# Down product of a two-layer encoder: the VectorE work of the Strassen items queued in the order of the program text

## The chip, the cores and the metric

The kernel runs on one core of a Trainium2 chip. The metric is the device time of one execution in microseconds (us). Before the change the median of 3 runs is 2260.68 us (2259.78 to 2261.06).

## The reference, cut to what matters

The reference is a trunk of two layers, each a mixer (an mLSTM, then a latent attention) and an MLP with a squared ReLU, on 1024 tokens of width 1024 in float32. The change lies in the second matrix product of the MLP:

```python
D_MODEL, SEQ, DEPTH = 1024, 1024, 2
D_FF = 4 * D_MODEL

def sq_relu_mlp(h, w1, w2):
    return jnp.square(jax.nn.relu(h @ w1)) @ w2

for layer in range(DEPTH):
    ...
    y = sq_relu_mlp(h, ffn_w1[layer], ffn_w2[layer])
    x = x + g2[:, None, :] * rms_norm(y, norm_g[layer, 3])
```

Here `h @ w1` is the up product (1024 x 1024 by 1024 x 4096) and the multiplication by `w2` (4096 x 1024) the down product. The trace shows one down product at about 801 to 1110 us and the other at about 1921 to 2258 us.

## The kernel before

**Three matmuls for one.** Every float32 operand is cut into a high part (an ACT cast, `uh`, `whi`) and a low part (a VectorE subtraction of the high part from the original, `ul`, `wlo`). `mm3` issues three matmuls of 128x128 by 128x512 for each product of tiles: high by high (L168), low weights by high activations (L169), and high weights by low activations (L170).

**Strassen items.** `mlp` (from L774) does the down product in 32 items: 8 groups `g` of two pairs of weight tiles each (`GP` = 2), and in each group 4 row blocks `j`. The first 28 items use a Strassen scheme of seven products, the last 4 (the group `ng - 1`) plain products. The products of an item come in the order s = 1, 6, 2, 3, 5, 4, 7 (loop variable `n`). Products 1 and 6 fill the two halves of one PSUM tile "mm" (128x1024), 2 and 3 the next, 4 and 7 the third; product 5 goes to a tile "sm" (128x512) that stays in PSUM for each `j` from the first group to the last and is never added on the way. Each "mm" tile takes 12 matmuls, product 5 takes 6, so an item has 42.

**Accumulators.** For each `j` there are three tiles "y" in SBUF: `c16`, `c23`, `c47`. After products 6, 3 and 7 `add` (L814) adds the "mm" tile into its accumulator: a VectorE addition of 128x1024 (L819), or an ACT copy (L817) in the first group. The pool of "mm" tiles has two buffers, so the matmuls of a tile cannot begin before the addition of the tile two before it has read the buffer.

**Activations.** `load` brings the tiles `u` of an item two items ahead; `cut_high` (L807, ACT) makes `uh` of the next item after product 1, `cut_low` (L813, two VectorE subtractions) makes `ul` after product 6.

**Weights.** The weights of later groups are prepared by generators (`w_pair` from L580, `w_plain` from L563 for the last group), which `w_step` moves on by one step after each product as long as room for tiles is left. For one pair of weight tiles the steps issue four GpSimd additions (L611, L612, L624, L631), ACT casts (L600, L636), three VectorE subtractions `wlo` (L604), and one VectorE subtraction for the tile `w4` of product 4 (L638). In `w_plain` the VectorE subtraction is L574.

**What sets the order.** A scheduler of the framework orders the instructions of each engine by a simulated timeline; a block under `tc.issue_after(X)` stays behind instruction X in the queue. Before the change only `cut_low` was held so: behind the instruction traced last, whichever it was. A helper `behind(*engines)` exists already; it looks up the last traced instruction of each engine named and holds what is traced in its block behind it. Additions, `wlo`, `w4` and the combining additions after the last Strassen group (L885, seven for each `j` when `g == ng - 2`) were ordered by the scheduler alone.

Of the kernel before, what the change touches and what calls it, by code (L numbers as in the profile page):

```python
# [65 lines left out]
class Trunk:  # L66
# [711 lines left out]
    def mlp(self, l, done, extra, last=None):  # L778

        S, V, G, GP, NP = self.S, self.V, self.G, self.GP, self.NP  # L780
# [5 lines left out]
        def load(it):  # L786
            if it < items:
                g, j = divmod(it, 4)
                loaded[it] = []
                for i in range(GP):  # L790
                    src = self.us[g * GP + i].rearrange("p (o j t) -> p o j t", o=8, j=4)[:, :, j]
                    if g == ng - 1:
                        if i == 0:
                            u = self.U("u")[:, : GP * 512]
                            loaded[it].append(u)
                        self.dma(out=u[:, i * 512 : (i + 1) * 512].rearrange("p (o t) -> p o t", o=4), in_=src[:, :4])
                    else:
                        u = self.U("u")[:, :896]
                        loaded[it].append(u)
                        self.dma(out=u.rearrange("p (o t) -> p o t", o=7), in_=src[:, 1:])  # L800

        def cut_high(it):
            if it < items:
                cuts[it] = []
                for u in loaded[it]:
                    x = tuple(v[:, : u.shape[-1]] for v in (self.U("uh", F32R), self.U("ul", F32R)))
                    S.copy(x[0], u)  # L807
                    cuts[it].append(x)

        def cut_low(it):  # L810
            if it < items:
                for u, x in zip(loaded.pop(it), cuts[it]):
                    V.tensor_tensor(out=x[1], in0=u, in1=x[0].bitcast(F32), op=ALU.subtract)  # L813

        def add(dst, ps, fresh=False):
            if fresh:
                S.copy(dst, ps)  # L817
            else:
                V.tensor_tensor(out=dst, in0=dst, in1=ps, op=ALU.add)  # L819
# [25 lines left out]
        for it in range(items - 4):  # L845
            g, j = divmod(it, 4)
            load(it + 2)
            c23, c47, c16 = acc[j]
            for n, (s, half) in enumerate(((1, 0), (6, 1), (2, 0), (3, 1), (5, None), (4, 0), (7, 1))):
                if half == 0:  # L850
                    both = self.MM()
                if half is None and g == 0:
                        fives[j] = self.SM()
                ps = fives[j] if half is None else both[:, (lo, hi)[half]]
                o = (self.US.index(self.LEFT[s]) - 1) * P
                start, stop = half is not None or g == 0, half is not None or g == ng - 2
                for i in range(GP):
                    key = (1, g * GP + i)
                    self.mm3(ps, tuple(u[:, o : o + P] for u in cuts[it][i]), self.w_take(key, s), start and i == 0, stop and i == GP - 1)
                    if j == 3:  # L860
                        self.w_used(key, s)
                if s == 6:
                    add(c16, both, g == 0)
                elif s == 3:
                    add(c23, both, g == 0)
                elif s == 7:
                    add(c47, both, g == 0)
                if n == 0:
                    cut_high(it + 1)
                elif n == 1:  # L870
                    with self.tc.issue_after(self.last()):
                        cut_low(it + 1)
                self.w_step(room=self.ROOM[1])
            del cuts[it]
            if g == ng - 2:
                for dst, src in (
                    (c16[:, hi], c16[:, lo]),
                    (c23[:, lo], c16[:, lo]),
                    (c47[:, hi], c16[:, hi]),
                    (c47[:, lo], c47[:, hi]),  # L880
                    (c47[:, hi], fives[j]),
                    (c16[:, hi], fives[j]),
                    (c23[:, hi], c16[:, hi]),
                ):
                    V.tensor_tensor(out=dst, in0=dst, in1=src, op=ALU.add)  # L885
                acc[j] = c23, c47
# [3 lines left out]
        for j in range(4):  # L890
# [3 lines left out]
            for row in (1, 0) if last and j == 3 else (0, 1):  # L894
                y = (even, odd)[row]
                both = self.MM()
# [1074 lines left out]
```

## Time and profile before

| What | Value |
|---|---|
| Median of 3 runs | 2260.68 us (2259.78 to 2261.06) |
| Profiled execution | 2259.8 us, of which span 2258.0 us |
| Mean granted TensorE clock | 0.996 |
| PE (TensorE matmuls) busy | 2200.4 us, 97% of the span |
| DVE (VectorE) busy | 1689.3 us, 75% |
| ACT (ScalarE) busy | 1013.2 us, 45% |
| POOL (GpSimd) busy | 458.1 us, 20% |

The profile comes from one execution. PE stands for TensorE's matmuls and PEld for its weight loads, DVE for VectorE, ACT for ScalarE, POOL for GpSimd, SP for the queue that issues DMAs. A line of a group names the line of the kernel, engine, operation, output and inputs, shapes, count, busy time in us, mean ns of one, and the idle time of the engine just before these instructions with what ended most of it. A line of the timeline gives start and duration in us, then the same names, "x2" for two in a row, and in brackets the idle time before and who ended it.

### The profile page before, as it was taken

The numbers are of one execution on the slowest core, as the hardware profiler recorded it, in microseconds if no ns is written. First come the engines' busy times: TensorE is split into PE (matmuls) and PEld (weight loads), VectorE is DVE, ScalarE is ACT, GpSimd is POOL, SyncE is SP. The second block draws the span as 40 slices with busy tenths as digits, with TensorE's granted clock in tenths as the row PEclk, the third lists the DMA queues.
The fourth block names the chain that finished last, engine by engine and source line by source line (L and its number), as shares of the span: only waits on it lengthen the run. The fifth ranks groups of instructions, "written<-read, shape, count | busy, mean of one in ns | idle before, by whom it ended". The sixth has DMA issues, their size and how long they took to land.

```text
span 2258.0 us, 28912 instructions
## 1 busy us (share of the span) xinstructions
PE 2200.4 (97%) x10814; PEld 1835.6 (81%) x10814; DVE 1689.3 (75%) x2503; ACT 1013.2 (45%) x1695; POOL 458.1 (20%) x309
## 2 busy tenths in 40 slices
PE   8999999999999999999999999999999999999998
PEld 6898888878778877777898989988787888777776
DVE  5677787567987768788988676664779776687888
ACT  4511445563444463333354445555634444633322
POOL 0000120004543434231000000000045433333300
PEclk9999999999999999999999999999999999999999
DMA  9487443245764554454321000113457545545452
GB/s 300 133 289 257 93 132 121 94 120 172 251 199 159 186 178 132 137 154 149 117 82 44 17 16 17 40 65 103 122 174 237 172 154 172 173 136 171 128 172 103
DMA packets 300068, 320.17 MB, mean 142 GB/s; under 512 B 16040, under 2 KB 252184, under 8 KB 299928
## 3 DMA queue, kind: packets, MB, share of 16 engines
q1 hardware_dynamic: 299928, 318.33, 44.7%
q8 instruction: 85, 1.39, 0.3%
q14 instruction: 55, 0.45, 0.1%
HBM read 245.85 MB, written 72.43 MB: 141 GB/s over the span
## 4 chain that ended last, share of the span: by engine, by line
PE 76%; DVE 14%; ACT 3%; issue 3%; DMA 3%; SPq 1%; DVEq 0%; POOL 0%; ACTq 0%; POOLq 0%
PE mm L168 14%; PE mm L170 14%; PE mm L169 14%; PE sm L168 10%; PE sm L169 10%; PE sm L170 10%; PE sm L208 3%; DVE wlo L604 2%; DVE ul L813 2%; DVE y L819 2%; DVE x L739 1%; DMA slab<-in_mod_w_dram 1%; DVE y L885 1%; DVE acc L298 1%; DMA modw<-in_mod_w_dram 1%
## 5 line engine op out<-in xcount | busy, mean ns | idle before, releaser
L168 PE MATMUL mm<-whi,uh 128*128 128x512 f32 x688 | 273.6, 398 | 14.5 <-DVE y L819 14.2
L169 PE MATMUL mm<-wlo,uh 128*128 128x512 f32 x688 | 271.0, 394 | 0.0
L170 PE MATMUL mm<-whi,ul 128*128 128x512 f32 x688 | 270.7, 394 | 0.0
L819 DVE TENSOR_TENSOR y<-y,mm 128x1024 f32<-128x1024 f32 (+1 forms) x161 | 192.6, 1208 | 86.3 <-PE mm L170 86.3
L631 POOL TENSOR_TENSOR tt<-raw,tt 128x512 f32<-128x512 f32 x60 | 113.6, 1893 | 616.4 <-DVE wlo L604 616.4
L168 PE MATMUL sm<-hSh,whi 128*128 128x512 f32 x560 | 223.0, 398 | 8.3 <-DVE x L739 8.0
L169 PE MATMUL sm<-hSl,whi 128*128 128x512 f32 x560 | 221.7, 396 | 0.0
L170 PE MATMUL sm<-hSh,wlo 128*128 128x512 f32 x560 | 219.9, 396 | 0.0
L739 DVE TENSOR_TENSOR x<-x,sm 128x512 f32<-128x512 f32 x198 | 132.3, 682 | 57.6 <-PE sm L170 54.3
L168 PEld LDWEIGHTS mm<-whi,uh 128*128 128x128 f32 x688 | 129.1, 188 | 53.7 <-DVE y L819 21.3
L813 DVE TENSOR_TENSOR ul<-u,uh 128x896 fp32r<-128x896 f32 (+1 forms) x120 | 153.5, 1318 | 24.9 <-ACT uh L807 24.9
L807 ACT CAST uh<-u 128x896 fp32r<-128x896 f32 (+1 forms) x120 | 109.6, 947 | 122.3 <-DVE ul L813 114.1
L611 POOL TENSOR_TENSOR tt<-raw,raw 128x512 f32<-128x512 f32 x32 | 64.8, 2025 | 486.0 <-DMA raw<-in_ffn_w_dram 480.2
L170 PEld LDWEIGHTS mm<-whi,ul 128*128 128x128 f32 x688 | 129.2, 188 | 30.3
L169 PEld LDWEIGHTS mm<-wlo,uh 128*128 128x128 f32 x688 | 129.2, 188 | 29.0
L604 DVE TENSOR_TENSOR wlo<-raw,whi 128x1024 fp32r<-128x1024 f32 x104 | 147.6, 1419 | 5.5 <-ACT whi L600 5.5
L168 PEld LDWEIGHTS sm<-hSh,whi 128*128 128x128 f32 x560 | 105.8, 189 | 36.4 <-DVE x L739 8.3
L742 ACT ACTIVATE x<-x 128x1024 f32<-128x1024 f32 x64 | 67.8, 1059 | 144.8 <-DVE x L739 144.5
L600 ACT CAST whi<-raw 128x1024 fp32r<-128x1024 f32 x104 | 108.7, 1045 | 42.7 <-DMA raw<-in_ffn_w_dram 21.3
L170 PEld LDWEIGHTS sm<-hSh,wlo 128*128 128x128 f32 x560 | 105.9, 189 | 25.1
L169 PEld LDWEIGHTS sm<-hSl,whi 128*128 128x128 f32 x560 | 105.9, 189 | 24.3
L298 DVE SCALAR_TENSOR_TENSOR acc<-modw,cact,acc 128x1024 f32<-128x1024 f32 x84 | 115.3, 1373 | 3.5 <-DMA modw<-in_mod_w_dram 2.6
(428 smaller groups left out, 5717.0 us busy)
## 6 DMA issues: line engine op xcount, KB each, us to landing
raw<-in_ffn_w_dram SPq DMA_DIRECT2D x144, 512.0 KB
u<-us SPq DMA_DIRECT2D x112, 448.0 KB
us<-x SPq DMA_DIRECT2D x92, 512.0 KB
modw<-in_mod_w_dram SPq DMA_DIRECT2D x80, 512.0 KB
x<-xn SPq DMA_DIRECT2D x24, 512.0 KB
x<-x SPq DMA_DIRECT2D x24, 512.0 KB
x<-in_x_dram SPq DMA_DIRECT2D x16, 512.0 KB
slab<-in_mod_w_dram SPq DMA_DIRECT2D x32, 256.0 KB
```

The source lines that it names most:

```text
L168: mm(out, a[0], b[0], start=start, stop=False)
L169: mm(out, a[0], b[1], start=False, stop=False)
L170: mm(out, a[1], b[0], start=False, stop=stop)
L298: self.V.scalar_tensor_tensor(out=acc, in0=t, scalar=self.cact[:, k : k + 1], in1=acc, op0=ALU.mult, op1=ALU.add)
L600: S.copy(x[0], u)
L604: V.tensor_tensor(out=x[1], in0=u, in1=x[0].bitcast(F32), op=ALU.subtract)
L631: G.tensor_tensor(out=t1, in0=b21, in1=t2, op=ALU.subtract)
L739: V.tensor_tensor(out=dst, in0=src, in1=ps, op=ALU.add)
L742: S.activation(u, u, AF.Relu)
L807: S.copy(x[0], u)
L813: V.tensor_tensor(out=x[1], in0=u, in1=x[0].bitcast(F32), op=ALU.subtract)
L819: V.tensor_tensor(out=dst, in0=dst, in1=ps, op=ALU.add)
```

## The change

The additions of the products, `cut_low`, and the step of the weight preparation after each product are all put under `behind(V)`, V being VectorE. Each block's VectorE instructions thereby stand in VectorE's queue behind the VectorE instruction that was traced last before the block. The instructions and their sizes stay the same; so do the additions at L885 themselves, which have no block of their own (they are at L887 afterwards, since two lines are added above them).

```diff
-                if s == 6:
-                    add(c16, both, g == 0)
-                elif s == 3:
-                    add(c23, both, g == 0)
-                elif s == 7:
-                    add(c47, both, g == 0)
+                with self.behind(V):
+                    if s == 6:
+                        add(c16, both, g == 0)
+                    elif s == 3:
+                        add(c23, both, g == 0)
+                    elif s == 7:
+                        add(c47, both, g == 0)
                 if n == 0:
                     cut_high(it + 1)
                 elif n == 1:
-                    with self.tc.issue_after(self.last()):
+                    with self.behind(V):
                         cut_low(it + 1)
-                self.w_step(room=self.ROOM[1])
+                with self.behind(V):
+                    self.w_step(room=self.ROOM[1])
```

VectorE's queue where one group ends and the next begins (item j = 3 of a group in the middle of the first layer, then j = 0 of the next group). The accumulators are y_1156 (`c23` of j = 3), y_1157 (`c47` of j = 3), y_1149 (`c16` of j = 0); mm_1267, mm_1272 and mm_1277 are the PSUM tiles of these three, in the order of their use:

```order
+L819 TENSOR_TENSOR y_1156_6934<-y_1156_6934,mm_1267_7468 128x1024
 L604 TENSOR_TENSOR wlo_1249_7353<-raw_1234_7291,whi_1248_7352 128x1024
 L604 TENSOR_TENSOR wlo_1269_7491<-tt_1247_7349,whi_1268_7490 128x1024
+L819 TENSOR_TENSOR y_1157_6935<-y_1157_6935,mm_1272_7497 128x1024
 L604 TENSOR_TENSOR wlo_1274_7505<-raw_1233_7289,whi_1273_7504 128x1024
-L819 TENSOR_TENSOR y_1156_6934<-y_1156_6934,mm_1267_7468 128x1024
-L819 TENSOR_TENSOR y_1157_6935<-y_1157_6935,mm_1272_7497 128x1024
-L638 TENSOR_TENSOR w4_1282_7534<-tt_1247_7349,w4_1282_7534 128x512
 L819 TENSOR_TENSOR y_1149_6927<-y_1149_6927,mm_1277_7521 128x1024
 L813 TENSOR_TENSOR ul_1279_7529<-u_1260_7442,uh_1278_7528 128x896
 L813 TENSOR_TENSOR ul_1281_7532<-u_1261_7444,uh_1280_7531 128x896
+L638 TENSOR_TENSOR w4_1282_7534<-tt_1247_7349,w4_1282_7534 128x512
```

The `c23` addition has moved ahead of three `wlo` subtractions and the `c47` addition ahead of one, and `w4` has moved behind the `c16` addition and the two `ul`. After this piece the `c23` addition of j = 0 (mm_1283) now stands ahead of wlo_1286 instead of behind it, and the `c47` addition (mm_1291) ahead of wlo_1293 instead of behind it.

TensorE's queue at the same place: mm_1277 is the tile of products 1 and 6 of j = 0, mm_1283 that of 2 and 3, mm_1291 that of 4 and 7 (from here the names end in further tiles of the two weight pairs):

```order
 L170 MATMUL mm_1283_7546<-whi_1248_7352,ul_1266_7457 128x512
+L169 MATMUL mm_1277_7521<-wlo_1274_7505,uh_1265_7456 128x512
+L170 MATMUL mm_1277_7521<-whi_1273_7504,ul_1266_7457 128x512
+L168 MATMUL mm_1277_7521<-whi_1231_7286,uh_1263_7453 128x512
+L169 MATMUL mm_1277_7521<-wlo_1232_7287,uh_1263_7453 128x512
+L170 MATMUL mm_1277_7521<-whi_1231_7286,ul_1264_7454 128x512
+L168 MATMUL mm_1277_7521<-whi_1268_7490,uh_1265_7456 128x512
+L169 MATMUL mm_1277_7521<-wlo_1269_7491,uh_1265_7456 128x512
+L170 MATMUL mm_1277_7521<-whi_1268_7490,ul_1266_7457 128x512
 L168 MATMUL mm_1291_7581<-w4_1245_7330,uh_1263_7453 128x512
 L169 MATMUL mm_1291_7581<-w4_1245_7330,uh_1263_7453 128x512
```

Before, these eight matmuls of mm_1277 stood ahead of the twelve of mm_1283; now they stand behind them and directly ahead of mm_1291, which uses the same PSUM buffer as mm_1277. Also, the four matmuls of product 5 of the next item that read its `ul` (sm_1191) stood behind all twelve of mm_1291 and now stand behind the first four of them. The full order from the tile of the ended item on is: before, mm_1272 x12, sm x6, mm_1277 x12, mm_1283 x12, mm_1291 x12, sm_1191 x4, mm_1296; after, mm_1272 x12, sm x2, mm_1277 x4, sm x4, mm_1283 x12, mm_1277 x8, mm_1291 x4, sm_1191 x4, mm_1291 x8, mm_1296.

VectorE's queue at the last Strassen group (j = 0), y_1149, y_1147 and y_1148 being `c16`, `c23` and `c47` of j = 0, y_1152 `c16` of j = 1:

```order
 L819 TENSOR_TENSOR y_1148_6926<-y_1148_6926,mm_1512_8726 128x1024
+L887 TENSOR_TENSOR y_1148_6926<-y_1148_6926,y_1149_6927 128x512
+L887 TENSOR_TENSOR y_1148_6926<-y_1148_6926 128x512
+L887 TENSOR_TENSOR y_1148_6926<-y_1148_6926,sm_1171_6988 128x512
+L887 TENSOR_TENSOR y_1149_6927<-y_1149_6927,sm_1171_6988 128x512
+L887 TENSOR_TENSOR y_1147_6925<-y_1147_6925,y_1149_6927 128x512
 L574 TENSOR_TENSOR wlo_1516_8745<-raw_1513_8733,whi_1515_8744 128x1024
-L887 TENSOR_TENSOR y_1147_6925<-y_1147_6925,y_1149_6927 128x512
-L887 TENSOR_TENSOR y_1148_6926<-y_1148_6926,y_1149_6927 128x512
 L819 TENSOR_TENSOR y_1152_6930<-y_1152_6930,mm_1519_8758 128x1024
```

Between the `c47` addition of j = 0 and the `c16` addition of j = 1 there stood one `wlo` and two combining additions; now five combining additions and the `wlo`. The order on ACT, POOL and SP is the same before and after.

## The prediction

> **What bounds the kernel now.** I read the busy times of the page first, then TensorE's list of waits over the whole run and over the first layer's down product (798 to 1112 us), then the stretches by engine, then the timelines of TensorE and VectorE at one place where a group of items ends.
>
> ```profile
> PE 2200.4 (97%) x10814; PEld 1835.6 (81%) x10814; DVE 1689.3 (75%) x2503; ACT 1013.2 (45%) x1695; POOL 458.1 (20%) x309
> L819 DVE TENSOR_TENSOR y<-y,mm 128x1024 f32<-128x1024 f32 (+1 forms) x161 | 192.6, 1208 | 86.3 <-PE mm L170 86.3
> ```
>
> ```profile
> PE mm L168 <- DVE y L819: 14.2, 17, 1.3
> ```
>
> ```profile
> PE mm L168 <- DVE y L819: 6.7, 8, 1.3
> PE mm L168 <- ACT y L817: 1.1, 1, 1.1
> ```
>
> TensorE is busy 97% of the span, so the change can only move TensorE's idle time. The change touches the down products alone, and there the waits are nearly all for the additions at L819 (in all 14.2 us in 17 waits; 6.7 us in 8 of them in the first layer). VectorE itself waits 86.3 us for matmuls in front of those additions, so it is not full on average, but the stretches show how much room it has:
>
> ```profile
> 964.00:1004.00 40.00, 39.21 (x168) 31.39 (x168) 32.12 (x29) 14.48 (x16) 13.10 (x9) 1.00 0.48 143
> 1044.00:1085.00 41.00, 38.29 (x162) 29.80 (x161) 39.59 (x46) 14.05 (x19) 0.90 (x1) 1.00 0.56 173
> ```
>
> The columns are the stretch, its length, then the busy time of PE, PEld, DVE, ACT and POOL, the granted clock, the DMA share and GB/s. A group of four items takes 40 us; VectorE works 32.12 us of it, TensorE 39.21. In the last Strassen group VectorE works 39.59 of 41 us: it is full there. Now the place where a group ends, first TensorE, then VectorE:
>
> ```profile
> 1002.10 0.40 PE L170 MATMUL mm<-whi,ul 128*128 128x512 f32 x1
> 1002.34 0.39 PE L170 MATMUL sm<-whi,ul 128*128 128x512 f32 x1
> ...
> 1003.50 0.40 PE L170 MATMUL sm<-whi,ul 128*128 128x512 f32 x1
> 1004.79 0.50 PE L168 MATMUL mm<-whi,uh 128*128 128x512 f32 x1 [0.90 <-DVE y L819]
> 1005.13 0.40 PE L169 MATMUL mm<-wlo,uh 128*128 128x512 f32 x1
> 1005.37 0.39 PE L170 MATMUL mm<-whi,ul 128*128 128x512 f32 x1
> ```
>
> ```profile
> 998.11 2.09 DVE L813 TENSOR_TENSOR ul<-u,uh 128x896 fp32r<-128x896 f32 x2
> 1000.12 1.22 DVE L604 TENSOR_TENSOR wlo<-raw,whi 128x1024 fp32r<-128x1024 f32 x1
> ...
> 1002.39 1.22 DVE L604 TENSOR_TENSOR wlo<-raw,whi 128x1024 fp32r<-128x1024 f32 x1
> 1003.52 2.35 DVE L819 TENSOR_TENSOR y<-y,mm 128x1024 f32<-128x1024 f32 x2
> 1005.79 0.77 DVE L638 TENSOR_TENSOR w<-tt,w 128x512 fp32r<-128x512 f32 x1
> 1007.88 1.22 DVE L819 TENSOR_TENSOR y<-y,mm 128x1024 f32<-128x1024 f32 x1 [1.33 <-PE mm L170]
> 1009.02 2.08 DVE L813 TENSOR_TENSOR ul<-u,uh 128x896 fp32r<-128x896 f32 x2
> ```
>
> The matmul at 1004.79 opens the next group's first tile and waits for the `c23` addition, which stands behind three `wlo` and ends at 1004.74. The down product of a layer has six ends of a group among its seven Strassen groups: the first (term 3), four of this kind (terms 1 and 2) and the last (term 4).
>
> **The step lengths.** From these rows: one matmul to the next 0.232 us (1002.34 to 1003.50 in five), but 0.34 after a stall; one addition or `wlo` to the next 1.13 (1000.12 to 1002.39 in two); an addition alone 1.22; two `ul` 2.01 (998.11 to 1000.12); a `w4` 0.77 alone (0.68 where an addition follows). TensorE starts 0.05 after the addition ends. How long after a tile's last matmul starts the addition does, shows this pair:
>
> ```profile
> 848.43 0.40 PE L170 MATMUL mm<-whi,ul 128*128 128x512 f32 x1
> ```
>
> ```profile
> 848.86 1.22 DVE L819 TENSOR_TENSOR y<-y,mm 128x1024 f32<-128x1024 f32 x1 [0.63 <-PE mm L170]
> 850.00 2.09 DVE L813 TENSOR_TENSOR ul<-u,uh 128x896 fp32r<-128x896 f32 x2
> ```
>
> 0.43 us. With these I replay the new order of the two queues by hand.
>
> **Term 1: the ordinary end of a group.** The new order does move the `c23` addition to 1000.12 (in front of the three `wlo`), and the first four matmuls of mm_1277 no longer wait. Ten matmuls then follow mm_1272 and the next, mm_1283, would start at 1002.34 + 10 x 0.232 = 1004.66. It needs the `c47` addition, now at 1000.12 + 3 x 1.13 = 1003.51, ended 1004.73: it starts at 1004.79, the very time of before. The last of its twelve starts at 1005.13 + 10 x 0.232 = 7.45 (from here us after 1000), the last of the eight of mm_1277 put behind it at 9.31. Then mm_1291 comes at once and needs mm_1277's buffer. The `c16` addition starts 9.31 + 0.43 = 9.74 and ends 10.96; mm_1291 would start at 9.54 and starts at 11.01: a wait of 1.47, with nothing between to hide it. Before, twelve matmuls (2.8 us) stood between the two tiles. Behind the addition stand the two `ul` (10.87 to 12.96), which product 5 of the next item needs after four plus three matmuls: wanted at 12.74, starts 13.01. Then `w4`, now last in the row, 12.88 to 13.65, which the next matmul of mm_1291 needs: wanted at 13.35, starts 13.70. With 0.11 for each restart mm_1291 ends its starts at 13.70 + 0.34 + 6 x 0.232 = 15.43, and mm_1296 opens at 15.66. Before it opened at 1005.13 + 39 x 0.232 = 14.18. So the end of a group costs **1.5 us more**, not less.
>
> **Term 2: what follows in the next item.** VectorE is late as well:
>
> ```profile
> 1017.15 1.22 DVE L819 TENSOR_TENSOR y<-y,mm 128x1024 f32<-128x1024 f32 x1 [0.38 <-PE mm L170]
> 1018.29 4.20 DVE L813 TENSOR_TENSOR ul<-u,uh 128x896 fp32r<-128x896 f32 x2
> 1022.41 0.68 DVE L638 TENSOR_TENSOR w<-tt,w 128x512 fp32r<-128x512 f32 x1
> 1023.01 2.34 DVE L819 TENSOR_TENSOR y<-y,mm 128x1024 f32<-128x1024 f32 x2
> ```
>
> ```profile
> 1024.40 0.39 PE L168 MATMUL mm<-whi,uh 128*128 128x512 f32 x1
> ```
>
> Before, the addition that frees the buffer of the matmul at 1024.40 ended at about 1024.2, just in time. After, `w4` at 12.88 is followed by `c23`, two `wlo`, `c47`, `wlo` and then the `c16` addition: 12.88 + 0.68 + 5 x 1.13 = 19.2 instead of 17.15. The same steps put the end of the `c23` addition at 24.2 + 2.05 = 26.25, where TensorE, 1.5 late, wants it at 25.9: a wait of 0.4 and a restart, some 0.5 us. Bounds: nothing, if the two `ul` (4.20 here, 2.09 above) are not slowed when they run later; and 1.1 more, if `w4` runs as in its slow row, 1.78 instead of 0.68:
>
> ```profile
> 857.67 3.19 DVE L813 TENSOR_TENSOR ul<-u,uh 128x896 fp32r<-128x896 f32 x2
> 860.79 1.78 DVE L638 TENSOR_TENSOR w<-tt,w 128x512 fp32r<-128x512 f32 x1
> 862.49 2.34 DVE L819 TENSOR_TENSOR y<-y,mm 128x1024 f32<-128x1024 f32 x2
> ```
>
> In both rows `ul` and `w4` together take 4.7 to 4.8 us, so I take the same again, **0.6**, with 0 and 1.7 as ends. Terms 1 and 2 apply to four ends of a group in each layer: 4 x 2.1 = 8.4.
>
> What slows the `ul` shows in GpSimd's rows of the same time:
>
> ```profile
> 1018.14 1.29 POOL L612 TENSOR_TENSOR tt<-raw,tt 128x512 f32<-128x512 f32 x1
> 1019.39 2.15 POOL L624 TENSOR_TENSOR raw<-raw,raw 128x512 f32<-128x512 f32 x1
> ```
>
> The first `ul` begins inside L612 and the second beside L624, and both stretch. GpSimd's additions follow the `wlo` and move with VectorE, so I leave the overlap as it is. [...]
>
> **Term 3: the first end of a group** (from ACT copies to additions). Before, `w4` and the `c23` addition were done ahead of the `c16` addition at 848.86; now `c16`, two `ul`, `w4`, `c23`. The next tile takes the buffer of the one that `c16` reads until 850.08: it starts at 850.13 instead of 849.13 (+1.0), then waits for `ul` at 852.1 (0.3) and for `w4` at 852.7 (0.3), with three restarts (0.3): **+1.9 us**. The stall that follows today at 863.75, behind the slow `w4` and the addition at 862.49, stays, both engines being as late as each other. Ends: 1.0 (the buffer alone) and 3.0 (`w4` slow as at 860.79).
>
> **Term 4: the last Strassen group.** The end of a group as in term 1, 1.5. Then the combining additions:
>
> ```profile
> L885 DVE TENSOR_TENSOR y<-y,y x24: 661/680/687, 1057.4 to 2211.8; 128x512 f32<-128x512 f32 x24
> ```
>
> ```profile
> 1066.46 1.21 DVE L819 TENSOR_TENSOR y<-y,mm 128x1024 f32<-128x1024 f32 x1
> 1067.59 1.88 DVE L885 TENSOR_TENSOR y<-y,y 128x512 f32<-128x512 f32 x3
> 1069.40 1.21 DVE L819 TENSOR_TENSOR y<-y,mm 128x1024 f32<-128x1024 f32 x1
> ```
>
> They follow one another in 0.60 us (1067.59 to 1069.40 in three). In the new order five instead of two stand ahead of the `c16` addition of j = 1, so it comes 1.8 us later, and VectorE has no room there (39.59 of 41). The replay through this group gives waits for additions of 0.6, 1.9, 0.5, 0.9 and 0.3 with five restarts of 0.11, 4.7 in all, where before there were four worth 2.9, the first and the last of them these:
>
> ```profile
> 1055.32 0.51 PE L168 MATMUL mm<-whi,uh 128*128 128x512 f32 x1 [0.38 <-DVE y L819]
> ...
> 1084.96 0.47 PE L168 MATMUL mm<-whi,uh 128*128 128x512 f32 x1 [1.34 <-DVE y L819]
> ```
>
> So 1.8 more, and **3.2** with the end of the group. Ends: 0.5 (VectorE's work is the same, so the group ends nearly when it did) and 5.
>
> The `w4` moved behind the `ul` at the start of the down product (804 to 813 us) I cost at nothing: TensorE waits there at 810 for the ACT copy at L817 in any case; without that cover it would be one `w4`, 0.7. The loads of `u` and GpSimd's work have two items of room. The four plain items are only shifted.
>
> **The sum.** Per layer 1.9 + 8.4 + 3.2 = 13.5, in two layers 27.0. On the profiled execution's own 2259.8 us that is 2286.8; the median of the runs is 0.9 above it, so 2288. With the low ends 1.0 + 4 x 1.5 + 0.5 = 7.5, twice 15: 2276. With the high ends 3.0 + 4 x 3.2 + 5 = 20.8, twice 41.6: 2302.
>
> **Rivals.**
> *Faster.* The additions come earlier and the waits for L819 go: 14.2 us with 17 restarts of 0.11 is 16.1, so 2244.6. For it: the `c23` addition does move from 1003.52 to 1000.12. Against it: it decides on whether 1.7 us of other matmuls (0.43 + 1.22 + 0.05) stand between mm_1277's last and mm_1291's first, and the order shows none. Chance 0.04.
> *No change.* TensorE has other matmuls in the waits, or the gain at `c23` is just given back: within 4.5 us of 2260.7. Against it: each engine's queue is in order. Chance 0.03.
> *A smaller loss.* Only term 1 holds, no wait in the next item, and the last group gives nothing: 2265 to 2276. Chance 0.10.
> *A larger loss.* VectorE, at 32 of 40 us a group, does not catch up in the three items behind a group's end, and the lateness is carried into the next end: if 1.5 us of it meets each of the eight next ends, 12 more, 2300; with slow `ul` and `w4` 2310. Chance 0.09. For it: term 2; against: VectorE has 8 us of idle time in a group.
>
> **How the numbers follow.** The forecast, 2276 to 2302 around 2288, has 0.74. A measurement of this kernel can tell about 0.2% (4.5 us) from no change. Faster is the first rival, 0.04; within 0.2% the second, 0.03; all the rest is slower, 0.93. The range is the forecast's own with 2 us more on each side, 2274 to 2304: it takes in the ends of the terms and part of the smaller and the larger loss, and leaves out some 0.2.
>
> **What would show it.** Right, if the profile after has, at each end of a group, TensorE waiting about 1.5 us for the `c16` addition (not `c23`), then short waits for `ul` L813 and `w4` L638, which do not occur now; if waits for L819 grow from 14.2 to some 30 us; and if in the last group `mm` waits stand behind runs of five L887. Term 2 is wrong if the matmul some 20 us after each end of a group does not wait. All of it is wrong if mm_1291 opens without a wait: then its buffer was another one. With all of TensorE's busy time unchanged (2200 us), any other difference must be in the clock, which is 1.00 in these stretches.

## The result and the profile after

The changed kernel takes 2289.14 us (median of 4 runs, 2287.77 to 2293.45), beside 2260.23 us for the kernel before in the same comparison: a ratio of 1.0131, 95% interval 1.0119 to 1.0142. The forecast was 2288 (2274 to 2304). The profiled execution took 2289.35 us with a span of 2287.5 us, 29.5 us more than the span before.

TensorE's list of waits of the changed kernel shows where the time is:

```profile
PE mm L168 <- DVE y L819: 29.3, 31, 2.3
PE sm L168 <- DVE x L739: 9.5, 10, 3.6
```

The waits for the additions have gone from 14.2 us in 17 to 29.3 us in 31. The next entry lies outside the down product; it was 8.0 us in 8 before the change.

The end of a group in the middle of the first layer (the same one as in the prediction; it now lies some 9 us later). TensorE's lines with a wait of at least 0.3 us:

```profile
1020.14 0.50 PE L168 MATMUL mm<-w,uh 128*128 128x512 f32 x1 [1.31 <-DVE y L819]
1035.69 0.50 PE L168 MATMUL mm<-whi,uh 128*128 128x512 f32 x1 [0.64 <-DVE y L819]
```

Two shorter waits follow the first of these, and the starts show them:

```profile
1021.71 0.40 PE L169 MATMUL sm<-wlo,uh 128*128 128x512 f32 x1
1022.14 0.50 PE L170 MATMUL sm<-whi,ul 128*128 128x512 f32 x1
1022.74 0.50 PE L169 MATMUL mm<-w,uh 128*128 128x512 f32 x1
```

VectorE at that place:

```profile
1018.86 1.22 DVE L819 TENSOR_TENSOR y<-y,mm 128x1024 f32<-128x1024 f32 x1 [3.69 <-PE mm L170]
1020.00 2.09 DVE L813 TENSOR_TENSOR ul<-u,uh 128x896 fp32r<-128x896 f32 x2
1022.00 0.68 DVE L638 TENSOR_TENSOR w<-tt,w 128x512 fp32r<-128x512 f32 x1
1022.60 1.22 DVE L819 TENSOR_TENSOR y<-y,mm 128x1024 f32<-128x1024 f32 x1
...
1028.46 1.21 DVE L819 TENSOR_TENSOR y<-y,mm 128x1024 f32<-128x1024 f32 x1
1029.60 3.20 DVE L813 TENSOR_TENSOR ul<-u,uh 128x896 fp32r<-128x896 f32 x2
1032.72 1.78 DVE L638 TENSOR_TENSOR w<-tt,w 128x512 fp32r<-128x512 f32 x1
1034.42 2.34 DVE L819 TENSOR_TENSOR y<-y,mm 128x1024 f32<-128x1024 f32 x2
```

The matmul at 1020.14 reads `w`, so it is the first of the tile of products 4 and 7, and it waits for the `c16` addition of 1018.86. VectorE waited 3.69 us in front of that addition, for TensorE: the addition could not start before the eight matmuls that the new order had put last. Each engine waits for the other in turn. The matmul at 1022.14 starts 0.05 us after the `ul` pair ends (1022.09), 0.43 us behind the matmul before it instead of 0.23, and the one at 1022.74 starts 0.06 after `w4` ends (1022.68), 0.60 behind. The matmul at 1035.69 waits for the first addition of 1034.42, behind an `ul` pair of 3.20 us and a `w4` of 1.78.

Stretches of the changed kernel (PE, PEld, DVE, ACT, POOL busy, granted clock, DMA share, GB/s):

```profile
1000.00:1040.00 40.00, 37.91 (x160) 29.09 (x159) 30.16 (x27) 13.77 (x15) 13.81 (x8) 1.00 0.47 145
1040.00:1080.00 40.00, 35.95 (x143) 27.08 (x142) 32.06 (x34) 14.08 (x16) 1.31 (x1) 0.96 0.41 125
```

In 40 us TensorE starts 160 matmuls instead of 168. VectorE is less busy than before (30.16 against 32.12): a group now takes 42.4 us instead of 40.1 (from the wait for `c16` at one end, 977.77, to that at the next, 1020.14), so less of its work falls into 40 us.

In the last Strassen group VectorE's lines around the combining additions are these:

```profile
1069.62 1.21 DVE L819 TENSOR_TENSOR y<-y,mm 128x1024 f32<-128x1024 f32 x1
1070.87 0.69 DVE L887 TENSOR_TENSOR y<-y,y 128x512 f32<-128x512 f32 x1
1071.59 0.69 DVE L887 TENSOR_TENSOR y<-y 128x512 f32<-128x512 f32 x1
1072.32 1.28 DVE L887 TENSOR_TENSOR y<-y,sm 128x512 f32<-128x512 f32 x2
1073.64 0.69 DVE L887 TENSOR_TENSOR y<-y,y 128x512 f32<-128x512 f32 x1
1074.25 1.22 DVE L574 TENSOR_TENSOR wlo<-raw,whi 128x1024 fp32r<-128x1024 f32 x1
1075.38 1.21 DVE L819 TENSOR_TENSOR y<-y,mm 128x1024 f32<-128x1024 f32 x1
```

Five additions and a `wlo` stand between the `c47` addition and the next `c16` addition, 5.76 us in all, and TensorE sits idle for 2.25 us until it is done (its lines stand at the end, with what happened behind that wait).

### The profile page after: what moved, and what is told of

Same layout as the page of the kernel before. It is cut to its first block, busy times and chain, and to the rows that moved or that the text cites. A ratio compares the mean times of both kernels' runs of the same rounds, so it can differ in the third digit from the quotient of the medians.

```text
span 2287.5 us, 28915 instructions
## 1 busy us (share of the span) xinstructions
PE 2213.9 (97%) x10814; PEld 1832.2 (80%) x10814; DVE 1694.1 (74%) x2503; ACT 1015.9 (44%) x1695; POOL 456.3 (20%) x309
## 4 chain that ended last, share of the span: by engine, by line
PE 65%; DVE 17%; issue 7%; DMA 5%; ACT 3%; POOL 2%; SPq 1%; DVEq 0%; POOLq 0%; ACTq 0%
PE mm L168 12%; PE mm L169 11%; PE mm L170 11%; PE sm L168 9%; PE sm L169 8%; PE sm L170 8%; DVE y L819 3%; DVE ul L813 3%; PE sm L208 3%; DVE wlo L604 2%; DMA u<-us 1%; DMA modw<-in_mod_w_dram 1%; DVE x L739 1%; DVE w L638 1%; DMA slab<-in_mod_w_dram 1%
## 5 line engine op out<-in xcount | busy, mean ns | idle before, releaser
L631 POOL TENSOR_TENSOR tt<-raw,tt 128x512 f32<-128x512 f32 x60 | 95.5, 1591 | 639.5 <-DVE wlo L604 639.5
L813 DVE TENSOR_TENSOR ul<-u,uh 128x896 fp32r<-128x896 f32 (+1 forms) x120 | 144.8, 1245 | 25.6 <-ACT uh L807 25.6
```

What stands on the lines that cost most here:

```text
L631: G.tensor_tensor(out=t1, in0=b21, in1=t2, op=ALU.subtract)
```

## The experiments

Nine kernels, each timed beside the kernel before on the same chip. Each diff is against the kernel that its text names. What a kernel costs more or less than another is taken from its distance to the kernel before in its own comparison. Where it says that TensorE loses some time, this is the sum of its distances from one start to the next above 0.30 us, less 0.23 each.

**1. Only the additions held** (against the changed kernel):

```diff
                 elif n == 1:
-                    with self.behind(V):
+                    with self.tc.issue_after(self.last()):
                         cut_low(it + 1)
-                with self.behind(V):
-                    self.w_step(room=self.ROOM[1])
+                self.w_step(room=self.ROOM[1])
```

> Only the additions are held in the order of the text; cut_low and the weight steps are as before. Theory (the hold on the weight steps reorders the ends of the groups, the hold on the additions acts only in the last Strassen group): at the ordinary ends the order is that of before, with the 1.3 us wait for the c23 addition; in the last group up to seven combining additions (0.60 each, 4.2 us) stand ahead of a c16 addition instead of three, so 2 to 3 us more per layer: about 2265 us (2260 to 2270). Rival (holding the additions costs the time): 2280 or more, with waits for c16 of 1.5 us at the ordinary ends.

Measured: 2266.89 us beside 2260.6, ratio 1.0027 (1.0017 to 1.0037). At the ordinary ends the queues stand as before and TensorE waits as before. The loss is in the last group, where the tiles of its third and fourth items wait 2.2 and 0.6 us. So the hold on the additions alone costs some 6 us, and not at the ordinary ends of the groups. The hold on `cut_low` alone was not run. In all groups but the first it names the same instruction as before the change, the `c16` addition traced just ahead of it, so little can hang on it.

**2. Only the weight steps held** (against the changed kernel): the additions without `behind(V)`, `cut_low` as before.

```diff
-                with self.behind(V):
-                    if s == 6:
-                        add(c16, both, g == 0)
...
+                if s == 6:
+                    add(c16, both, g == 0)
...
```

> Only the weight steps are held; additions and cut_low are as before. Theory: at each ordinary end the eight late matmuls of the first tile still stand directly ahead of the tile that takes its buffer, so the wait of 1.5 us for the c16 addition is there, but the scheduler fills the waits for ul and w4 with matmuls of the next item: an end costs about 1.2 us more than before instead of 2.2; eight ends 9.6, the first ends 2, the last groups 2 to 6: about 2275 us (2268 to 2284). Rival (holding the additions costs the time): within 5 us of before, 2256 to 2265.

Measured: 2276.25 us beside 2260.6, ratio 1.0070 (1.0055 to 1.0085). This hold alone costs 16 us, and the rival falls. But the expected wait of 1.5 us for `c16` at the tile of products 4 and 7 isn't there. In this kernel the scheduler puts the `c23` addition of the item ahead of its `c16` addition (VectorE adds at 1011.50 and 1013.36, 0.42 and 0.43 us after the start of the last matmul of the second tile's twelve and of the first tile's late eight), the tile of products 4 and 7 opens without a wait, and it is the next item's first tile that waits for `c16`, 0.79 us from start to start instead of 0.23. That the two tiles have changed buffers is what these waits say; I read it from them alone. The wait for `ul` has not gone either, as TensorE's list of waits shows:

```profile
PE mm L168 <- DVE y L819: 9.2, 25, 1.0
PE mm L170 <- DVE ul L813: 7.5, 14, 2.2
```

Behind the wait for `c16` the third matmul waits for `ul` (0.67 from start to start), and in the last group the wait for `ul` is 2.16 us. An ordinary end, with the next item, loses 2.1 us here, 1.2 before the change and 3.4 in the changed kernel. The holds of experiments 1 and 2 add up to 22 of the 29 us; the rest comes only where both are held.

**3. TensorE held in the order of the text as well** (against the changed kernel):

```diff
-                    self.mm3(ps, tuple(u[:, o : o + P] for u in cuts[it][i]), self.w_take(key, s), start and i == 0, stop and i == GP - 1)
+                    w = self.w_take(key, s)
+                    with self.behind(*((self.PE,) if j == 0 and s == 2 and i == 0 else ())):
+                        self.mm3(ps, tuple(u[:, o : o + P] for u in cuts[it][i]), w, start and i == 0, stop and i == GP - 1)
```

> The changed kernel, with one hold more, on TensorE: in the first item of each group the matmuls of product 2 stay behind those of product 6, so that the tile of products 1 and 6 is finished before the next one is begun. VectorE's order stays that of the changed kernel. Theory (the wait comes from a tile's last matmuls standing directly ahead of the tile that takes its buffer): twelve matmuls (2.8 us) then cover the c16 addition; the eight matmuls wait 1.2 us for the third wlo instead, ul and w4 are done in time, an end costs 0.2 more than before instead of 2.2, and some 16 us of the 29 go: about 2270 us (2264 to 2276). Rival (VectorE is late at the ends whichever way TensorE's queue stands, w4 and ul behind c16): 2283 or more.

Measured: 2271.82 us beside 2260.6, ratio 1.0052 (1.0033 to 1.0071): some 17 of the 29 us go, with VectorE's order at the ends unchanged. TensorE's waits at the same end of a group:

```profile
1007.79 0.50 PE L169 MATMUL mm<-wlo,uh 128*128 128x512 f32 x1 [1.25 <-DVE wlo L604]
1027.07 0.50 PE L168 MATMUL mm<-whi,uh 128*128 128x512 f32 x1 [0.47 <-DVE y L819]
```

The first is the wait for the third `wlo`, as worked out (1.2), and the wait of 1.31 for `c16` and those for `ul` and `w4` are gone. The second was not expected: the wait in the next item has shrunk from 0.64 to 0.47 and not gone. So an ordinary end, with the next item, still loses 2.3 us, 1.1 more than before and not 0.2, and the eight of them give back 9 us and not 16; the rest comes from the first ends (3.4), the last groups (2.9) and the start of the down products (1.2), which the expectation had left out. The total was met by luck. What the run does show is that more than half of the loss hangs on TensorE's own order: the matmuls of a tile put directly ahead of the tile that takes its buffer.

**4. `w4` free again** (against the changed kernel):

```diff
-                with self.behind(V):
+                with self.behind(*((V,) if j or n > 1 else ())):
                     self.w_step(room=self.ROOM[1])
```

> The changed kernel without the hold on the weight steps after products 1 and 6 of the first item of a group, so w4 stands again ahead of the c16 addition. Theory: the wait for c16 stays at 1.5 us, the waits for ul (0.3) and w4 (0.5) go, VectorE is 0.7 us less late and the wait in the next item (0.9) goes: an end costs about 0.65 more than before instead of 2.2, the first end of a group nothing; what is left is mostly the last groups: about 2273 us (2268 to 2278). Rival (the place of w4 is a trifle, only its 0.5 goes at ten ends): 2283 or more.

Measured: 2270.07 us beside 2260.6, ratio 1.0043 (1.0029 to 1.0058), and the rival falls. The total is as worked out, but the way to it is the other one:

```profile
1026.79 0.50 PE L168 MATMUL mm<-whi,uh 128*128 128x512 f32 x1 [1.16 <-DVE y L819]
```

The wait for `c16` at the end of the group is gone and the one in the next item is larger (1.16 instead of 0.64). As in experiment 2, the scheduler now places the `c23` addition of the item ahead of `c16`. VectorE is still late behind the end, and TensorE, no longer delayed as much, runs into that lateness. The size was right for a wrong reason: the run shows that 19 us hang on the place of `w4`, but not through the waits that were expected to go. These 19 and the 17 of experiment 3 are more than 29 together, so they are not separate shares: either change alone takes away much of the same loss.

**5. No holds in the last Strassen group** (against the changed kernel): both `behind(V)` around the additions and the weight steps become

```diff
-                with self.behind(V):
+                with self.behind(*((V,) if g < ng - 2 else ())):
```

> The changed kernel with the holds on additions and weight steps lifted in the last Strassen group (the group of the combining additions). Theory: there the c16 additions no longer stand behind five combining additions, the wait of 2.3 us and the slow matmuls after it in the first layer go, and ul and w4 no longer hold TensorE at the last end: 2 to 4.5 us per layer less than the changed kernel, about 2282 us (2278 to 2286); granted clock 1.00 in every stretch of the last group. Rival (VectorE is full in this group, so the order of its work changes nothing): 2287 to 2290.

Measured: 2282.92 us beside 2261.11, ratio 1.0093 (1.0077 to 1.0109): 21.8 us more than the kernel before instead of 28.9, so 7.1 less, 3.5 a layer. The stretch that showed a clock of 0.96 has 1.00 again:

```profile
1040.00:1080.00 40.00, 38.53 (x165) 30.26 (x164) 34.01 (x35) 15.01 (x16) 1.30 (x1) 1.00 0.49 148
1080.00:1120.00 40.00, 38.01 (x163) 30.21 (x162) 40.00 (x66) 10.44 (x20) 0.00 (x0) 1.00 0.33 109
```

VectorE is full (40.00 of 40) here too, so being full did not make the order of its work indifferent.

**6. One GpSimd subtraction left out** (against the changed kernel):

```diff
-        G.tensor_tensor(out=b12, in0=b22, in1=b12, op=ALU.subtract)
+        if i == 0:
+            G.tensor_tensor(out=b12, in0=b22, in1=b12, op=ALU.subtract)
```

> The changed kernel with one GpSimd subtraction per pair of down weights left out (L624, which makes the weight of product 7; that weight then stays the plain one). All orders stay. [...]

Measured: 2283.88 us beside 2261.11, ratio 1.0098 (1.0084 to 1.0112): 22.8 us more than the kernel before instead of 28.9, so 6.1 less. Expected were about 2281 us (2279 to 2284), 6 to 9 less than the changed kernel, from a `ul` pair and a `w4` 1.1 to 1.2 us shorter together at the item after each end. VectorE and GpSimd behind the end of the group (the lines from L631 on are one higher here):

```profile
1026.24 3.19 DVE L814 TENSOR_TENSOR ul<-u,uh 128x896 fp32r<-128x896 f32 x2
1029.35 0.68 DVE L639 TENSOR_TENSOR w<-tt,w 128x512 fp32r<-128x512 f32 x1
1029.95 2.34 DVE L820 TENSOR_TENSOR y<-y,mm 128x1024 f32<-128x1024 f32 x2
```

```profile
1026.43 2.05 POOL L612 TENSOR_TENSOR tt<-raw,tt 128x512 f32<-128x512 f32 x1
```

With the GpSimd subtraction gone, `w4` takes 0.68 instead of 1.78 with the same operands, and TensorE no longer waits in the next item, where it waited 0.64 us. The `ul` pair keeps its 3.19; another GpSimd addition (L612, 2.05 us) still runs beside it. How a GpSimd addition comes to slow VectorE's work, no run shows.

**7. The `c23` addition first, nothing else** (against the kernel before):

```diff
-                self.w_step(room=self.ROOM[1])
+                with self.behind(*((V,) if j == 3 and n in (3,) else ())):
+                    self.w_step(room=self.ROOM[1])
```

> The kernel of before with a single hold: in the last item of a group the weight step after product 3 stays behind the c23 addition, so VectorE does c23, three wlo, c47, w4 instead of three wlo, c23, c47, w4; the tiles of TensorE keep their order, but two blocks of product 5 stand between the first four and the last eight matmuls of the first tile. Theory (the gain at c23 is real, it was lost to the order of the rest): the first tile no longer waits 0.9 us for c23, its last eight wait 0.15 for the third wlo: an end costs 0.9 less than before; eight ends 7.5, and up to 2 at the last ends, where VectorE is full: about 2252 us (2249 to 2256). Rival (the wait only moves from c23 to the next thing that VectorE owes): within 3 us of before, 2257 to 2263.

Measured: 2263.0 us beside 2261.11, ratio 1.0010 (1.0002 to 1.0019). The expected gain of 8 us is not there. The wait at the first tile has gone and stands 40 matmuls later:

```profile
1016.82 0.50 PE L168 MATMUL mm<-whi,uh 128*128 128x512 f32 x1 [0.85 <-DVE y L819]
```

VectorE's lines in between, GpSimd's and ACT's:

```profile
1009.15 1.11 DVE L638 TENSOR_TENSOR w<-tt,w 128x512 fp32r<-128x512 f32 x1 [0.70 <-ACT w L636]
1010.19 1.21 DVE L819 TENSOR_TENSOR y<-y,mm 128x1024 f32<-128x1024 f32 x1
1011.32 3.18 DVE L813 TENSOR_TENSOR ul<-u,uh 128x896 fp32r<-128x896 f32 x2
```

```profile
1006.26 2.21 POOL L631 TENSOR_TENSOR tt<-raw,tt 128x512 f32<-128x512 f32 x1 [21.24 <-DVE wlo L604]
...
1011.38 2.17 POOL L624 TENSOR_TENSOR raw<-raw,raw 128x512 f32<-128x512 f32 x1
```

```profile
1008.50 0.62 ACT L636 CAST w<-tt 128x512 fp32r<-128x512 f32 x1 [4.91 <-POOL tt L631]
```

GpSimd's L631 waits for the second `wlo`, which the `c23` addition has pushed back. ACT's cast for `w4` waits for L631, and VectorE's `w4` for the cast (0.70); and L624 now falls on the `ul` pair, which takes 3.18 instead of 2.08. The 0.9 us won at `c23` comes back as 0.85 at the next `c23`; with some shorter waits an ordinary end loses 1.7 us, 1.2 before.

**8. Only the third `wlo` behind `c23`** (against the kernel before):

```diff
+                if n == 3:
+                    mark = self.last()
+                with ExitStack() as pins:
+                    if j == 3 and n == 6:
+                        pins.enter_context(self.tc.issue_after(mark))
+                    self.w_step(room=self.ROOM[1])
-                self.w_step(room=self.ROOM[1])
```

> The kernel of before with a single hold: in the last item of a group only the third wlo (traced in the weight step after product 7) stays behind the c23 addition. VectorE then does two wlo, c23, the third wlo, c47, w4; TensorE's queue at the ends is that of before. Theory (in the run with c23 ahead of all three wlo the gain came back because the second wlo releases GpSimd's chain, which was 1.1 us or more later and then made w4 wait and stretched the ul): here GpSimd's chain starts when it did, c23 ends at the very time TensorE wants the tile, the last eight matmuls wait 0.15 for the third wlo. Some of the 0.9 per end comes back through ul beside L624 (up to 0.4): eight ordinary ends give 4 to 7 us: about 2255 us (2252 to 2258). Rival (VectorE owes the same sum of work before the c23 addition of the next item, so any gain comes back): 2259 to 2263, with a wait of about 1 us at the 37th matmul of the new group.

Measured: 2256.83 us beside 2259.88, ratio 0.9982 (0.9973 to 0.9991): faster than the kernel before, if only by 3 us (0.2%, with the interval clear of 1), and within the expected 2252 to 2258. GpSimd's chain starts as it did before, right behind the second `wlo`, and the long waits at the ends are gone:

```profile
1002.21 1.29 POOL L631 TENSOR_TENSOR tt<-raw,tt 128x512 f32<-128x512 f32 x1 [20.11 <-DVE wlo L604]
```

```profile
PE mm L168 <- DVE y L819: 5.3, 7, 1.4
```

The waits for additions fall from 14.2 us to 5.3. The whole gain is smaller than that, since the third `wlo` is now waited for at ten places by about 0.3 us and a restart: TensorE loses 18.0 us in the two down products where it lost 22.8.

**9. Experiment 7 without L624** (the diff of 6 on top of 7):

> The kernel with c23 ahead of the three wlo, and without GpSimd's subtraction L624 (the weight of product 7 then stays the plain one). Theory: the two ul after the first c16 addition of a group no longer run beside L624 (3.18 to 2.1 us), so the c23 addition of the new item comes 1.1 us earlier, the wait of 1.0 us at the tile of the next item goes, and so does part of the following one: 7 to 11 us less than with L624, about 2253 us (2250 to 2257). Rival (w4, which waits 0.7 us for GpSimd's L631 and its ACT copy, sets the rest): L624 is not on that way, so 2260 to 2263.

Measured: 2252.63 us beside 2259.88, ratio 0.9970 (0.9957 to 0.9983): 7 us less than the kernel before, where experiment 7 took 2 more, so 9 us hang on L624.

```profile
1002.77 1.13 DVE L639 TENSOR_TENSOR w<-tt,w 128x512 fp32r<-128x512 f32 x1 [0.71 <-ACT w L637]
1003.82 1.21 DVE L820 TENSOR_TENSOR y<-y,mm 128x1024 f32<-128x1024 f32 x1
1004.95 2.08 DVE L814 TENSOR_TENSOR ul<-u,uh 128x896 fp32r<-128x896 f32 x2
```

`w4` still waits 0.71 us for the cast, but the `ul` pair is back at 2.08 and the wait in the next item is gone. So in experiment 7 the gain was lost to the GpSimd addition beside `ul`, and not to the wait for the cast. The kernel before without L624 was not run, so it is not shown what L624 costs where `c23` is not pulled forward.

## Why the prediction was right, and where its terms were off

The direction, the size and the mechanism held: 28.9 us more by the medians, 27 forecast. Each term is sized by what TensorE loses at the place in both traces, counted as in the experiments.

- **Term 1, the ordinary end.** Forecast +1.5; measured 1.2 lost before and 2.5 after, so +1.3. Each of the four parts of the replay is there: a trifle at the second tile (0.1), the wait for `c16`, then `ul` and `w4`. Experiment 3 shows the cause: without the eight matmuls in front of it, that wait goes.
- **Term 2, the next item.** Forecast +0.6 with 0 and 1.7 as ends; measured +0.9, in all eight places. The replay itself came to a wait of 0.4 and a restart, 0.5; the measured wait is 0.8 and a restart. The slowing of `ul` and `w4` was taken over rightly: from start to start they took 4.82 us (1029.60 to 1034.42), as in the slow row shown. Counted from the start of the tile of products 2 and 3 (1004.79 in the replay, 1013.89 in the trace), the `c23` addition ended 0.3 us later than in the replay, 0.2 of it at the `wlo` ahead of the `c16` addition (1.32 us to the next start instead of 1.13), and TensorE wanted the buffer 0.1 earlier. Experiment 6 shows that the GpSimd addition beside `w4` makes the wait: in the changed kernel `w4` takes 1.78 us beside L624 (1031.81 to 1033.95), without L624 it takes 0.68, and there is no wait.
- **Term 3, the first end.** Forecast +1.9; measured 2.8 against 0.8, +1.95.
- **Term 4, the last group.** Forecast +3.2; measured 8.3 against 4.0 in the first layer and 8.2 against 4.0 in the second, +4.3 and +4.2. The end of the group was as in term 1 (+1.4). Behind it, the second layer shows all five waits of the replay, delays of 0.5, 2.4, 0.5, 1.1 and 0.6 us where it had 0.6, 1.9, 0.5, 0.9 and 0.3. Half of the difference comes from the combining additions: in the new order four of the five read what the addition ahead wrote and come 0.12 us later (0.72 from 1070.87 to 1071.59, where the replay had 0.60; the one that does not, the second of the pair at 1072.32, follows at 0.60), so the `c16` addition came 0.5 later (5.76 us behind the `c47` addition instead of 5.26). The rest lies in the waits of the two items behind it. In the first layer the granted clock was 0.55 for 3.8 us after the long wait (2.25 us) and the matmuls there lost 1.7 us more, but the waits behind it were shorter for it (0.3 and 0.6 instead of 0.5, 1.1 and 0.6), so the layer lost no more than the second.

Per layer the measured terms are 1.95 + 4 x 2.2 + 4.25 = 15.0, in two layers 30, against 29.5 in the spans. That the sum came so close is in part luck: term 1 was 0.2 too large and term 2 was 0.3 too small at each of the eight ends.

Of the rivals, *faster* fell as it was put: no other matmuls stood between the two tiles of one buffer. Its seed was true, though: the `c23` addition did come earlier, and where nothing else is moved with it (experiment 8) the kernel is a little faster. *A smaller loss* fell too: the next item waits in all eight places, and the last groups lose over 4 us each. *The larger loss* did not come: each end of a group looks like the one before, so VectorE's lateness doesn't add up.

Open stays which tile takes which buffer in experiments 2 and 4, which I only read from the waits.

## What to carry to other kernels

A hold that puts one engine's queue in the order of the text also reorders the engines that wait for it: look up what the other queue now puts directly ahead of the tile that reuses a buffer, and price the wait for the whole way matmul, addition, matmul (0.43 + 1.22 + 0.05 = 1.7 us here). With two PSUM buffers the last matmuls of a tile stood directly ahead of the tile after the next here, which cost a wait of 1.31 us at the end of the group; experiment 3, which put twelve others between, took back 17 of the 29 us. When an operation is pulled forward, ask which other engine was released by the operations it passes; here that was GpSimd, whose delayed additions gave the gain back by slowing VectorE (in experiment 7 the `ul` pair took 3.18 us beside L624 instead of 2.08, and without L624 the kernel took 9 us less).

## What the runs showed of the hardware that was not expected

A wait of TensorE of 2.25 us was followed by 3.8 us of matmuls at a granted clock of 0.55. In the changed kernel, first layer, behind the wait for the `c16` addition:

```profile
1076.65 0.61 PE L168 MATMUL mm<-w,uh 128*128 128x512 f32 x1 [2.25 <-DVE y L819]
1077.07 0.63 PE L169 MATMUL mm<-w,uh 128*128 128x512 f32 x1
...
1080.05 0.53 PE L170 MATMUL mm<-whi,ul 128*128 128x512 f32 x1
1080.42 0.40 PE L168 MATMUL mm<-whi,uh 128*128 128x512 f32 x1
```

```profile
1076.60:1080.40 3.80, 3.75 (x9) 2.92 (x10) 3.80 (x4) 1.68 (x2) 0.00 (x0) 0.55 0.46 137
```

In the stretch the matmuls follow at 0.43 us instead of 0.23. That is 1.7 us lost by these matmuls, but the group does not end later for it: the same wait in the second layer was followed by matmuls at 0.23 and a granted clock of 1.00 (2210.57 to 2214.40), and TensorE lost as much there in longer waits for VectorE (8.2 us in the last group, against 8.3 in the first layer).

```profile
2210.57 0.50 PE L168 MATMUL mm<-w,uh 128*128 128x512 f32 x1 [2.25 <-DVE y L819]
2210.91 0.39 PE L169 MATMUL mm<-w,uh 128*128 128x512 f32 x1
```

In experiments 3, 4 and 6, too, only the first layer had slow matmuls, and its last group lost just 0.1 us more than the second layer's; in experiment 1, where the second layer had them, it lost 0.8 us more than the first.

In the six profiles that have such a wait in the last group (the changed kernel and experiments 1, 2, 3, 4 and 6, two layers each, 2.5 to 2.7 us from start to start), 7 of 12 were followed by matmuls at 0.43; no wait of 1.8 us or less in the down products was. No threshold can be read from this: outside the down products the granted clock also was 0.50 behind a shorter wait, of 1.80 us, in experiment 1:

```profile
84.24 0.22 PE L208 MATMUL sm<-ident,posf 8*128 8x8 f32 x1 [1.80 <-DVE posf L1468]
```

```profile
85.50:88.90 3.40, 3.40 (x14) 3.40 (x13) 3.26 (x14) 1.43 (x2) 0.41 (x4) 0.50 1.08 311
```
